# Layer 1's input projection by seven products of quarters in place of eight

## The chip, the cores and the metric

The kernel runs on one core of a Trainium2 chip. The metric is the device time of one execution in microseconds (us), the median of several runs; lower is better. A trace of one execution, taken by the profiler of the hardware, stands beside it.

## What is computed

Two layers of a diffusion trunk over L = 1024 tokens with D = 2048 channels, in float32. Layer 0 is an attention layer, layer 1 a pooling layer. Cut to what the change touches, layer 1 is:

```python
h = _rmsnorm(x, pre_g) * (1 + scale) + shift                 # (1024, 2048)
proj = h @ w_in                                              # w_in: (2048, 4096)
# four groups of 512 channels: centred means over 2, 4, 8, 16 tokens minus the token
pooled = multiscale(proj[..., :2048])
mixed = einsum('blgc,gcd->blgd', pooled, pool_w) * pool_scale  # pool_w: four of (512, 512)
y = mixed * silu(proj[..., 2048:])
x = x + gate * _rmsnorm(y @ w_out, post_g)
```

The first 2048 columns of `w_in` give the values, the last 2048 the gates.

## The kernel before, in words

Every float32 product is made of three TensorE passes over a high and a low part (`PASSES`): `split` casts a tile to the high part on ScalarE (L144) and subtracts it on VectorE for the low part (L147). Weights come by `w_tiles` as raw tiles `wr` of 512 KB (two buffers, SP's DMA queue), each split into two tiles `wh`, `wl` (four buffers of each); a matmul multiplies a 128x128 block of weights with 512 tokens and adds into one PSUM bank `g`. `load` is a DMA on SP's queue, `store` one on ScalarE's. GpSimd (POOL) issues no DMA and no DMA accumulates. A scheduler orders the instructions of each engine from the program's order and its own estimate of times; places named `pin` or `keep_in_program_order` are held.

Layer 0's attention runs in 32 units: 16 of dense attention, then 16 of windowed. Each unit loads `qt`, `zt` and, by way of DRAM (`lsd`), a broadcast of its row sums `rs`; GpSimd multiplies `zt` by `rs` (L857), VectorE multiplies the output by that (`y`, L863), and the result goes to DRAM (`yd`).

Layer 0's output projection (`out_proj`, L953) runs over two halves n of 512 tokens. After each half, its rows are normalised (`add_norm`), transposed (L1053), scaled (`nw`) and split into 16 operand tiles `hT[k][n]`. While the second half is normalised, TensorE works on `first_gates`: the gates of six blocks of 128 columns for the first half of the tokens (`BRIDGE`, 288 matmuls, L1034), with the transposes between them, and their SiLU goes to DRAM (`sd`).

Then, for each of four groups of 512 channels: `project1` makes the values of two blocks of 128 columns at a time, for both halves of the tokens (L184, names `g`), `pooled` makes the centred means of them (adds on VectorE and GpSimd in turn, L1097), `project1` makes the gates, the group's product with `pool_w` (`mx`, L184) is multiplied by the SiLU of the gates (L1128), and the result `yt` goes to DRAM. Layer 1's output projection follows (L953).

## Time and profile before

| | us |
|---|---|
| median of 3 runs | 3043.45 (3042.88 to 3043.84) |
| the profiled execution | 3042.5 |
| its span, first to last instruction | 3040.8 |
| TensorE busy | 2951.6 (97%), 14038 matmuls |
| VectorE busy | 1612.4 (53%) |
| ScalarE busy | 1067.0 (35%) |
| GpSimd busy | 169.3 (6%) |

The busy times are those of the span of the profiled execution; engines work side by side, so they don't add up to it. The DMA share is the mean busy share of the core's 16 DMA engines.

### The profile page before, as it was taken

To read this page: it belongs to the slowest core of one execution; us is meant where nothing else is said; L and a number is where in the kernel's file an instruction comes from. 1 tells how busy PE (TensorE), PEld (TensorE's weight loads), DVE (VectorE), ACT (ScalarE), POOL (GpSimd) and SP (SyncE) were. 2 spreads that over 40 slices of the span, in tenths; PEclk is the share of its full clock that TensorE was granted. 3 is DMA by queue.
4 is the path that set the end of the run, shared out by engine and by line. 5 is a ranking of instruction groups with operands and counts; after the bars stand their busy time and mean duration, and the time that the engine had idled before them with its cause. 6 is when DMAs were issued, how large, how long until landed. Compare 5 with 4: busy or idle time off the path is not lost.

```text
span 3040.8 us, 38187 instructions
## 1 busy us (share of the span) xinstructions
PE 2951.6 (97%) x14038; PEld 2456.4 (81%) x14038; DVE 1612.4 (53%) x2866; ACT 1067.0 (35%) x2060; POOL 169.3 (6%) x150
## 2 busy tenths in 40 slices
PE   5999999999999999999899999999999999999998
PEld 4788888778887878888778888888888888888887
DVE  7979875663347478888633543533333323233434
ACT  5553322211212267766632443522222212122322
POOL 0000000000000000002200210300000002000000
PEclk8999999999999999999999999999999999999999
DMA  8858878886668554446554635414122121454634
GB/s 314 291 179 258 257 238 260 280 291 218 210 220 298 178 151 142 115 150 167 143 188 157 237 97 170 150 49 143 45 95 76 63 90 49 151 191 146 252 109 163
DMA packets 373009, 530.32 MB, mean 174 GB/s; under 512 B 28644, under 2 KB 215894, under 8 KB 371670
## 3 DMA queue, kind: packets, MB, share of 16 engines
q1 hardware_dynamic: 287990, 445.81, 45.5%
q10 hardware_dynamic: 84832, 82.07, 7.9%
q8 instruction: 110, 1.80, 0.2%
q14 instruction: 77, 0.63, 0.1%
HBM read 428.88 MB, written 98.91 MB: 174 GB/s over the span
## 4 chain that ended last, share of the span: by engine, by line
PE 80%; DMA 11%; DVE 5%; issue 2%; ACT 1%; POOL 0%; SPq 0%; ACTq 0%; DVEq 0%; POOLq 0%
PE g L184 41%; PE g L953 21%; DMA mraw<-in_od_mod_w_dram 5%; PE o L895 4%; PE mx L184 3%; PE s L252 3%; PE t L841 3%; DVE mac L345 2%; PE g L1034 2%; DMA mraw<-in_ev_mod_w_dram 2%; DMA lsd<-ls 1%; DMA rs<-lsd 1%; DMA wr<-in_od_w_out_dram 1%; PE c L258 1%; DMA zt<-in_ctx_dram 1%
## 5 line engine op out<-in xcount | busy, mean ns | idle before, releaser
L147 DVE TENSOR_TENSOR wl<-wr,wh 128x512 fp32r<-128x512 f32 (+1 forms) x576 | 395.8, 692 | 843.2 <-ACT wh L144 831.1
L144 ACT CAST wh<-wr 128x512 fp32r<-128x512 f32 (+1 forms) x576 | 350.5, 616 | 1152.3 <-PE g L184 584.3
L184 PE MATMUL g<-h,wh 128*128 128x512 f32 x2368 | 743.0, 394 | 1.9 <-ACT h L144 1.8
L953 PE MATMUL g<-wh,a 128*128 128x512 f32 x1920 | 593.7, 390 | 0.4 <-ACT wh L144 0.4
L184 PE MATMUL g<-a,wh 128*128 128x512 f32 x1856 | 571.2, 389 | 0.0
L184 PEld LDWEIGHTS g<-h,wh 128*128 128x128 f32 x2368 | 445.3, 190 | 93.6 <-ACT h L144 2.5
L184 PE MATMUL g<-h,wl 128*128 128x512 f32 x1184 | 465.0, 393 | 5.0 <-DVE wl L147 5.0
L953 PEld LDWEIGHTS g<-wh,a 128*128 128x128 f32 x1920 | 360.2, 188 | 75.1 <-ACT wh L144 0.8
L345 DVE SCALAR_TENSOR_TENSOR mac<-mraw,csil,mac 128x512 f32<-128x512 f32 x480 | 357.1, 748 | 112.6 <-DMA mraw<-in_od_mod_w_dram 61.1
L184 PEld LDWEIGHTS g<-a,wh 128*128 128x128 f32 x1856 | 348.4, 188 | 72.3
L953 PE MATMUL g<-wl,a 128*128 128x512 f32 x960 | 373.7, 389 | 0.0
L184 PE MATMUL g<-a,wl 128*128 128x512 f32 x928 | 360.7, 389 | 0.0
L184 PEld LDWEIGHTS g<-h,wl 128*128 128x128 f32 x1184 | 224.4, 190 | 53.0 <-DVE wl L147 6.5
L953 PEld LDWEIGHTS g<-wl,a 128*128 128x128 f32 x960 | 180.2, 188 | 37.5
L184 PEld LDWEIGHTS g<-a,wl 128*128 128x128 f32 x928 | 174.2, 188 | 36.3
L147 DVE TENSOR_TENSOR tl<-t,th 128x512 fp32r<-128x512 f32 x236 | 160.0, 685 | 39.2 <-ACT th L144 37.8
L144 ACT CAST th<-t 128x512 fp32r<-128x512 f32 x236 | 135.9, 585 | 111.3 <-PE t L841 110.3
L895 PE MATMUL o<-th,vt 128*128 128x512 f32 x472 | 156.2, 412 | 2.5 <-ACT th L144 2.5
L841 PE MATMUL t<-ident,p 128*128 128x128 f32 x944 | 138.9, 276 | 10.2 <-DVE tl L147 9.8
L841 PEld LDWEIGHTS t<-ident,p 128*128 128x128 f32 x944 | 114.4, 141 | 38.1 <-DVE tl L147 15.6
L857 POOL TENSOR_TENSOR zt<-zt,rs 128x512 f32<-128x512 f32 x32 | 49.6, 1552 | 1426.0 <-DMA zt<-zd 1075.5
L252 PE MATMUL s<-kt,qt 128*128 128x512 f32 x384 | 103.4, 404 | 0.0
(216 smaller groups left out, 3002.6 us busy)
## 6 DMA issues: line engine op xcount, KB each, us to landing
mraw<-in_ev_mod_w_dram SPq DMA_DIRECT2D x192, 256.0 KB, 4.2
mraw<-in_od_mod_w_dram SPq DMA_DIRECT2D x192, 256.0 KB, 4.2
wr<-in_od_w_in_dram SPq DMA_DIRECT2D x76, 512.0 KB, 3.7
wr<-in_ev_w_in_dram SPq DMA_DIRECT2D x68, 512.0 KB, 4.7
mraw<-in_ev_mod_w_dram SPq DMA_DIRECT2D x64, 512.0 KB, 4.7
wr<-in_ev_w_out_dram SPq DMA_DIRECT2D x64, 512.0 KB, 3.7
wr<-in_od_w_out_dram SPq DMA_DIRECT2D x64, 512.0 KB, 5.2
qd<-hl ACTq DMA_DIRECT2D x64, 256.0 KB, 3.9
```

What stands on the lines that cost most here:

```text
L144: nc.scalar.copy(dst_h, src)
L147: (lo or nc.vector).tensor_tensor(dst_l, src, f32(dst_h), op=ALU.subtract)
L184: pin(nc.tensor.matmul(o, lhsT=w[a][:, kk, m * P : (m + 1) * P], rhs=rhs(n, k, b), start=(k == 0 and i == 0), stop=(k == kc - 1 and i == 2),))
L252: pin(nc.tensor.matmul(s[:, sl], lhsT=qt[:, h, a], rhs=kt[:, b, sl], start=i == 0, stop=i == 2))
L258: pinned(nc.tensor.matmul(cs[:, hh], lhsT=qt[:, h + hh, a], rhs=kt[:, b, L:], start=i == 0, stop=i == 2))
L345: nc.vector.scalar_tensor_tensor(a, w, c, a, op0=ALU.mult, op1=ALU.add)
L841: pin(nc.tensor.transpose(t[:, h * P : (h + 1) * P], ps[h][:, i * P : (i + 1) * P], ident))
L857: GATE.tensor_tensor(zt, zt, rs.rearrange("p q h -> p h q"), op=ALU.mult)
L895: pin(nc.tensor.matmul(outs[u], lhsT=vt[:, a, kb], rhs=b, start=(i == 0 and jj == 0), stop=(last and jj == 2)))
L953: nc.tensor.matmul(o, lhsT=y[k][:, a, t * P : (t + 1) * P], rhs=wt[b][:, k - k0, :], start=(k == 0 and i == 0), stop=(k == KC - 1 and i == 2),
L1034: mm = nc.tensor.matmul(o, lhsT=w[a][:, k - k0, m * P : (m + 1) * P], rhs=hT[k][0][:, b], start=(k == 0 and i == 0), stop=(k == KC - 1 and ...
```

## The change

One level of a seven-product scheme (Strassen's, with Winograd's sums) replaces the eight products of layer 1's input projection. The tokens' channels are cut into X11, X12 (first 512 tokens; channels 0 to 1023 and 1024 to 2047) and X21, X22 (last 512 tokens), the weights into W11, W12, W21, W22 (channels by values or gates). `quarter(a, b, q, c)` is 512 KB of W: four 128-row blocks of half q of row quarter a, 256 columns of block c of column quarter b. Each product is 1024 channels x 2048 columns x 512 tokens.

- `early_sums`, in the attention units: for the first four of eight column blocks c and both q, sums of quarters of W11, W12 and W22 are made by DMA (load one quarter, then `accum_op=add` DMAs on GpSimd's queue) and stored to DRAM as `td` (three quarters) and `te` (two quarters),; every sign of the scheme is in the sums of tokens.
- `first_products` takes the place of `first_gates`: X11 W11 goes into PSUM, is copied out (`p1d`), and X12 W21 goes on top of it; the result `ud` is the values of the first 512 tokens. Two quarters of weights (24 matmuls) stand between two transposes. Four VectorE subtractions per channel block make the operand tiles of the later products; three of the five are spilled to DRAM (`opd`).
- `second`, a stage with its own pool and a ring of six raw tiles: product 3 with W12+W11+W22 (`td`), minus `p1d`, is stored as `u2d`; product 4 with W22+W12 (`te`) goes on top in PSUM, minus `p1d`, is stored as `u3d`. For c from 4 on the sums are made here.
- The third stage reloads three sets of eight operand tiles (`reloaded`), and makes for each group the values of the last 512 tokens (X22 with `td`+W21), the gates of the last and, on top in PSUM, those of the first 512 tokens. The product with `pool_w` of a group runs after the values of the next group, for each half of the tokens apart, so `pool_w` is loaded twice. All pooling adds are VectorE's.
- Layer 0's first half of the output projection casts its operand tiles on ScalarE, no longer on GpSimd, and stores them to DRAM as `xd` too.

```diff
+OG = 16
+EARLY = 4
+BETWEEN = 2
+PL = 3
+RING = 6
...
+    w_in1 = ins["od_w_in"][0]
+    def quarter(a, b, q, c):
+        r = (8 * a + 4 * q) * P
+        return w_in1[r : r + 4 * P, b * D + c * 256 : b * D + (c + 1) * 256].rearrange("(k p) m -> p k m", p=P)
...
+        early = []
+        def early_sums(u):
+            c, q, step = u // 8, u // 4 % 2, u % 4
+            if c >= EARLY:
+                return
+            dma = nc.gpsimd.dma_start
+            if step == 0:
+                early[:] = [ap.tile([P, 4, 256], F32, tag=tag, name=tag, bufs=1) for tag in ("qa", "qb")]
+                for r, b in zip(early, (0, 1)):
+                    load(r, quarter(b, 1, q, c))
+            elif step == 1:
+                for r, b in zip(early, (0, 1)):
+                    dma(out=r, in_=quarter(0, b, q, c), accum_op=ALU.add)
+            elif step == 2:
+                load(te[q][c], early[1])
+                dma(out=early[0], in_=quarter(1, 1, q, c), accum_op=ALU.add)
+            else:
+                load(td[q][c], early[0])
...
+            early_sums(u)
...
+    raw_tiles = [lambda: wp.tile([P, 1024], F32, tag="wr", name="wr", bufs=2)]
+    raws_made, ring = [0], [2]
+    def quarter_tiles(src):
+        for q in range(2):
+            i = raws_made[0] % ring[0]
+            raws_made[0] += 1
+            raw = raw_tiles[i > 1]()
+            r = raw.rearrange("p (k m) -> p k m", k=4)
+            first, *others = src(q)
+            load(r, first)
+            for o in others:
+                if o[0] == "store":
+                    store(o[1], r)
+                else:
+                    nc.gpsimd.dma_start(out=r, in_=o[1], accum_op=ALU.add)
+            for i in range(2):
+                h = wp.tile([P, WT], F32R, tag="wh", name="wh", bufs=WB)
+                l = wp.tile([P, WT], F32R, tag="wl", name="wl", bufs=WB)
+                split(h, l, raw[:, i * WT : (i + 1) * WT])
+                yield 4 * q + 2 * i, 2, [t.rearrange("p (k m) -> p k m", k=2) for t in (h, l)]
+    def sum_of(c, *quarters, kept=None, more=None):
+        def at(q):
+            r = [quarter(a, b, q, c) for a, b in quarters]
+            if more:
+                r.insert(0, more[q][c])
+            return [r[0], *(("add", o) for o in r[1:]), *([("store", kept[q][c])] if kept else [])]
+        return at
+    def products(outs, group, op, first, pin=lambda i: i):
+        for m, o in enumerate(outs):
+            for k0, nk, w in group:
+                for k in range(k0, k0 + nk):
+                    for i, (a, b) in enumerate(PASSES):
+                        pin(nc.tensor.matmul(
+                            o, lhsT=w[a][:, k - k0, m * P : (m + 1) * P], rhs=op(k)[:, b],
+                            start=(first and k == 0 and i == 0), stop=(k == 7 and i == 2), skip_group_check=not first,
+                        ))
...
+        def first_products():
+            def part(c, outs, i):
+                for k0, nk, w in quarter_tiles(sum_of(c, (i, 0))):
+                    products(outs, [(k0, nk, w)], lambda k: hT[8 * i + k][0], i == 0, tc.keep_in_program_order)
+                    yield
+            def evicted(c, outs, d):
+                for m, o in enumerate(outs):
+                    t = ev.tile([P, HL], F32, tag="pe", name="pe", bufs=2)
+                    nc.scalar.copy(t, o)
+                    store(d[2 * c + m], t)
+            held = {}
+            for c in range(9):
+                if c < 8:
+                    held[c] = [psg.tile([P, HL], F32, tag="g", name="g") for _ in range(2)]
+                    yield from part(c, held[c], 0)
+                    evicted(c, held[c], p1d)
+                if c:
+                    outs = held.pop(c - 1)
+                    yield from part(c - 1, outs, 1)
+                    evicted(c - 1, outs, ud)
...
+        early = first_products()
+        list(islice(early, LEAD))
+        ops = [[None] * 8 for _ in range(2)]
+        for k in range(8):
+            x11 = ev.tile([P, HL], F32, tag="x11", name="x11", bufs=2)
+            x12 = ev.tile([P, HL], F32, tag="gp", name="x12", bufs=1)
+            load(x11, xd[k])
+            load(x12, xd[k + 8])
+            ws = []
+            for kk in (k, k + 8):
+                list(islice(early, BETWEEN))
+                ws.append(columns_of(1, kk, og))
+            x21, x22 = ws
+            s3 = ev.tile([P, HL], F32, tag="s3", name="s3", bufs=1)
+            nc.vector.tensor_tensor(s3, x21, x11, op=ALU.subtract)
+            nc.vector.tensor_tensor(x21, x21, x22, op=ALU.subtract)
+            nc.vector.tensor_tensor(x11, x11, x21, op=ALU.subtract)
+            nc.vector.tensor_tensor(x12, x12, x11, op=ALU.subtract)
+            for i, a in enumerate((x11, s3)):
+                ops[i][k] = acts[1, i].tile([P, 2, HL], F32R, tag="a", name="a")
+                operand(ops[i][k], a)
+            for i, a in enumerate((x22, x21, x12)):
+                store(opd[i][k], a)
+        list(early)
...
+        ready = [fetched(p1d[m]) for m in range(2)]
+        def second(c, outs, accumulate):
+            if c < EARLY:
+                src = sum_of(c, more=(td, te)[accumulate])
+            else:
+                src = sum_of(c, (1, 1), (0, 1)) if accumulate else sum_of(c, (0, 1), (0, 0), (1, 1), kept=td)
+            product(outs, src, ops[accumulate], not accumulate)
+            for m, o in enumerate(outs, 2 * c):
+                p = ready.pop(0) if ready else fetched(p1d[m])
+                nc.vector.tensor_tensor(p, o, p, op=ALU.subtract)
+                store((u2d, u3d)[accumulate][m], p)
+        held = {}
+        for c in range(9):
+            if c < 8:
+                held[c] = pair()
+                second(c, held[c], 0)
+            if c:
+                second(c - 1, held.pop(c - 1), 1)
...
+        def reloaded(i, n, half):
+            r = []
+            for k in range(8):
+                t = acts[n, half].tile([P, 2, HL], F32R, tag="a", name="a")
+                w = fetched(opd[i][k])
+                split(t[:, 0], t[:, 1], w)
+                r.append(t)
+            return r
+        x22, s1t, s4t = reloaded(0, 1, 0), reloaded(1, 0, 0), reloaded(2, 0, 1)
...
+        def values(g, c2):
+            c, outs = 2 * g + c2, pair()
+            product(outs, sum_of(c, (1, 0), more=td), x22)
+            r = []
+            for m, o in enumerate(outs, 2 * c):
+                u = us[m % 2]
+                load(u[:, PAD : PAD + HL], ud[m])
+                nc.vector.tensor_tensor(u[:, PAD + HL : PAD + L], o, fetched(u3d[m]), op=ALU.subtract)
+                r.append(pooled(g, m, u))
+            return r
+        def gates(g, c2, outs, n):
+            c = 2 * g + c2
+            if n:
+                product(outs, sum_of(c, (0, 1), (0, 0)), s1t)
+            else:
+                product(outs, sum_of(c, (1, 1)), s4t, False)
+            for m, o in enumerate(outs, 2 * c):
+                p = fetched((u2d, u3d)[n][m])
+                nc.vector.tensor_tensor(p, o, p, op=ALU.add)
+                nc.scalar.activation(p, p, AF.Silu)
+                store(sd[m][n], p)
...
+        mixes = []
         for g in range(4):
+            po = values(g, 0) + values(g, 1)
+            for f in mixes:
+                f()
+            held = [pair(), pair()]
+            for n in (1, 0):
+                for c2 in range(2):
+                    gates(g, c2, held[c2], n)
+            mixes = [lambda g=g, cc=cc, n=n, po=po: mixed(g, cc, n, po) for n in range(NH) for cc in (0, 2)]
+        for f in mixes:
+            f()
```

GpSimd's queue at the start of the dense attention units, before (only the products of `zt` and `rs`):

```order
L857 TENSOR_TENSOR zt_9186<-zt_9186,rs_8993 128x512 [waits DMAHW0_49,DMAHW7_49,DVE_49,PE_49]
L857 TENSOR_TENSOR zt_9400<-zt_9400,rs_9219 128x512 [waits DMAHW6_49]
L857 TENSOR_TENSOR zt_9615<-zt_9615,rs_9434 128x512 [waits DMAHW4_49,DMAHW3_49,DVE_49]
```

Each row is one unit's product. With the change, in the same place (the DMA rows accumulate into `qa` and `qb`):

```order
L896 TENSOR_TENSOR zt_9340<-zt_9340,rs_9147 128x512 [waits DMAHW1_49,DMAHW2_49,DVE_49,PE_49]
L864 DMA qa_9368<-in_od_w_in_dram 128x4x256 [waits DMAHW3_49,DVE_49]
L864 DMA qb_9369<-in_od_w_in_dram 128x4x256 [waits DMAHW4_49,DVE_49,PE_49]
L867 DMA qa_9368<-in_od_w_in_dram 128x4x256 [waits DMASW0_49]
L864 DMA qb_10237<-in_od_w_in_dram 128x4x256 [waits DMAHW5_49,DMAHW3_49,DMASW1_49]
L896 TENSOR_TENSOR zt_9558<-zt_9558,rs_9377 128x512 [waits DMAHW4_49,DMAHW1_49]
L864 DMA qa_10236<-in_od_w_in_dram 128x4x256 [waits DMAHW5_49,DMAHW1_49,DMASW2_49]
L867 DMA qa_10236<-in_od_w_in_dram 128x4x256 [waits DMASW4_49]
L864 DMA qb_11112<-in_od_w_in_dram 128x4x256 [waits DMAHW6_49,DMAHW0_49,DMASW3_49]
L896 TENSOR_TENSOR zt_9775<-zt_9775,rs_9594 128x512 [waits DMAHW1_49,DVE_49]
```

Three accumulating DMAs and one product of a unit now alternate in one queue, and the second DMA into the same buffer waits for the first.

SP's queue in the second dense unit and after it, before (issued loads and stores of the attention):

```order
L240 DMA qt_9621<-qd0_1_109 128x1024 [waits DMAHW0_49,PE_49]
L856 DMA zt_9830<-zd0_0_116 128x512 [waits DMAHW1_49,DVE_49]
L287 DMA lsd2_126<-ls_9194 128x4 [waits DMAHW2_49,DVE_49,Activation_49]
L867 DMA yd0_0_156<-yo_9423 512x1x128 [waits DMAHW3_49,Activation_49]
L909 DMA rs_9434<-lsd2_126 128x512 [waits DMAHW2_49]
L867 DMA yd0_0_156<-yo_9423 512x1x128 [waits DMAHW5_49,DVE_49]
```

The unit's own transfers follow one another. With the change, the same place reads:

```order
L259 DMA qt_9564<-qd0_0_108 128x1024 [waits DMAHW4_49,PE_49]
L866 DMA te0_0_196<-qb_9369 128x1024 [waits DMAHW5_49,DMASW1_49]
L895 DMA zt_9775<-zd0_0_116 128x512 [waits DMAHW6_49,DVE_49]
L306 DMA lsd1_125<-ls_9169 128x4 [waits DMAHW7_49,DVE_49,Activation_49]
L906 DMA yd0_0_156<-yo_9363 512x1x128 [waits DMAHW0_49,Activation_49]
L869 DMA td0_0_180<-qa_9368 128x1024 [waits DMAHW1_49,DMASW2_49]
L906 DMA yd0_0_156<-yo_9363 512x1x128 [waits DMAHW2_49,DVE_49]
L861 DMA qb_10237<-in_od_w_in_dram 128x4x256 [waits DMAHW5_49,DMAHW3_49]
L948 DMA rs_9377<-lsd1_125 128x512 [waits DMAHW7_49,DMAHW4_49]
L861 DMA qa_10236<-in_od_w_in_dram 128x4x256 [waits DMAHW1_49]
L866 DMA te1_0_200<-qb_10237 128x1024 [waits DMAHW6_49,DMASW3_49]
```

The stores of `te` and `td` and the loads of the next quarters now stand between `zt`, `lsd`, `yd` and `rs`, and each waits for a DMA of GpSimd's queue (DMASW) or for a buffer.

SP's queue around the load of `edge`, where layer 1's groups begin, before:

```order
L160 DMA wr_18148<-in_od_w_in_dram 128x4x256 [waits DMAHW1_49,DVE_49]
L160 DMA wr_18206<-in_od_w_in_dram 128x4x256 [waits DMAHW6_49,DMAHW2_49,DVE_49]
L1067 DMA edge_18023<-in_edge_dram 128x64 [waits DMAHW7_49]
L1127 DMA zt_18760<-sd0_180 128x512 [waits Pool_49]
L160 DMA wr_18298<-in_od_w_in_dram 128x4x256 [waits DMAHW3_49,DVE_49]
L160 DMA wr_18356<-in_od_w_in_dram 128x4x256 [waits DMAHW6_49,DVE_49]
```

The weight loads of the first group run on through it. With the change, at the start of the third stage (`pl` from `opd` are the reloads of X22's operand tiles, from `p1d` those of the second stage):

```order
L1062 DMA wr_20527<-td0_0_180 128x1024 [waits DMASW6_49,DVE_49]
L1195 DMA pl_20389<-p1d15_259 128x512 [waits DMAHW6_49,DMAHW5_49,DVE_49]
L1062 DMA wr_20562<-td1_0_188 128x1024 [waits DMASW7_49,DVE_49]
L1062 DMA wr_20745<-in_od_w_in_dram 128x4x256 [waits DMAHW1_49,DMASW0_49,DVE_49]
L1062 DMA wr_20780<-in_od_w_in_dram 128x4x256 [waits DMAHW4_49,DMASW1_49,DVE_49]
L1232 DMA edge_20397<-in_edge_dram 128x64 [waits DMAHW2_49]
L1195 DMA pl_20406<-opd0_0_220 128x512 [waits DMAHW6_49,DMASW5_49,DMASW2_49]
L1195 DMA pl_20411<-opd0_1_221 128x512 [waits DMAHW7_49,DMASW3_49]
L1195 DMA pl_20416<-opd0_2_222 128x512 [waits DMAHW0_49]
L1286 DMA u0_20399<-ud0_292 128x512 [waits DMAHW3_49,DMAHW1_49]
```

The reloads of X22 now stand behind four loads of weight tiles into two `wr` buffers.

## Rows read from the trace of the kernel before

**Rows 1.** The page: the span, TensorE's busy time, the 40 slices of clock and DMA.
```profile
span 3040.8 us, 38187 instructions
PE 2951.6 (97%) x14038; PEld 2456.4 (81%) x14038; DVE 1612.4 (53%) x2866; ACT 1067.0 (35%) x2060; POOL 169.3 (6%) x150
...
PEclk8999999999999999999999999999999999999999
DMA  8858878886668554446554635414122121454634
```

**Rows 2.** The chain that ended last, from 1888 us: start us, us, what.
```profile
1888.50 39.44 PE g L1034 x174
1928.38 1.38 PE g L1034 x6
...
1962.72 107.21 PE g L184 x473
2069.94 11.19 PE mx L184 x48
2081.13 21.77 PE g L184 x96
...
2681.81 85.03 PE g L953 x375
```

**Rows 3.** Windows: stretch, its us, busy us (instructions) by engine, clock, DMA share, GB/s.
```profile
1093.00:1260.00 167.00, 166.36 (x950) 137.63 (x949) 139.54 (x241) 118.25 (x242) 13.99 (x9) 1.00 0.44 127
1888.50:2069.90 181.40, 181.40 (x833) 150.38 (x833) 83.37 (x170) 72.40 (x137) 28.41 (x34) 1.00 0.32 104
1888.50:2681.80 793.30, 793.30 (x3521) 655.01 (x3521) 274.23 (x463) 207.18 (x360) 66.58 (x66) 1.00 0.29 95
2300.00:2320.00 20.00, 20.00 (x90) 16.56 (x89) 2.07 (x3) 1.47 (x4) 0.00 (x0) 1.00 0.18 53
```

**Rows 4.** The page: SP's DMA queue: packets, MB, share of 16 engines' span.
```profile
q1 hardware_dynamic: 287990, 445.81, 45.5%
```

**Rows 5.** DMA issues: out<-in, queue, number, KB each, median us to landing.
```profile
wr<-in_od_w_in_dram SPq DMA_DIRECT2D x76, 512.0 KB, 3.7
qt<-qd SPq DMA_DIRECT2D x32, 512.0 KB, 8.5
...
y1d<-yt ACTq DMA_DIRECT2D x32, 512.0 KB, 2.6
...
rs<-lsd SPq DMA_DIRECT2D x32, 256.0 KB, 3.7
zt<-zd SPq DMA_DIRECT2D x32, 256.0 KB, 3.0
...
zt<-sd SPq DMA_DIRECT2D x6, 256.0 KB, 4.6
```

**Rows 6.** Timeline of SP, one issue in an attention unit: start us, us, what.
```profile
1096.77 0.32 SPq L909 DMA_DIRECT2D rs<-lsd  x1
```

**Rows 7.** Timeline of VectorE, the gated outputs of two attention units.
```profile
1111.42 0.68 DVE L863 TENSOR_TENSOR y<-o,zt 128x512 f32<-128x512 f32 x1
...
1129.93 0.68 DVE L863 TENSOR_TENSOR y<-o,zt 128x512 f32<-128x512 f32 x1
```

**Rows 8.** Timeline of GpSimd (POOL) in the same units.
```profile
1100.24 1.56 POOL L857 TENSOR_TENSOR zt<-zt,rs 128x512 f32<-128x512 f32 x1 [22.70 <-DMA rs<-lsd]
1120.35 1.55 POOL L857 TENSOR_TENSOR zt<-zt,rs 128x512 f32<-128x512 f32 x1 [18.55 <-DMA rs<-lsd]
```

**Rows 9.** Groups by line and shape: shapes, count, busy us, mean ns, idle before.
```profile
L147 DVE TENSOR_TENSOR wl<-wr,wh 128x512 fp32r<-128x512 f32 x544 | 378.1, 700 | 835.8 <-ACT wh L144 823.8 <-DMA a<-y1d 8.8 <-DMA hc<-hcd 0.9
L144 ACT CAST wh<-wr 128x512 fp32r<-128x512 f32 x544 | 334.3, 622 | 1101.0 <-PE g L184 553.1 <-PE g L953 305.3 <-DMA wr<-in_ev_w_out_dram 49.3
...
L1128 DVE SCALAR_TENSOR_TENSOR zt<-mx,v,zt 128x512 f32<-128x512 f32 x32 | 24.0, 751 | 39.9 <-PE mx L184 31.6 <-DMA zt<-sd 7.4 <-ACT zt L1080 0.9
L1097 DVE TENSOR_TENSOR s<-u 128x543 f32<-128x543 f32 x32 | 23.1, 721 | 40.1 <-ACT u L1087 39.4
```

More of the change, by code (lines that the diff above doesn't have):

```diff
@@ L45 @@
 LAST = "TTPATTAPTPPTTPATPTPTPPNP"
-BRIDGE = 6
 PINS = (0,)
@@ new lines, in operand @@
+        def operand(o, w):
+            split(o[:, 0], o[:, 1], w)
+        og = out_proj(ev, ins["ev_w_out"][0], ys[0], gpd[0], 0, lambda t: x[t * P : (t + 1) * P, :], add_norm, other_half(yd))
+        for k in range(KC):
+            w = columns_of(0, k, og)
+            store(xd[k], w)
+            hT[k][0] = act_tile(k, 0)
+            operand(hT[k][0], w)
+        og = out_proj(ev, ins["ev_w_out"][0], ys[1], gpd[0], 1, lambda t: x[t * P : (t + 1) * P, :], add_norm)
+        early = first_products()
@@ new lines, in tile_backbone, with etile, fetched, pair @@
+        list(early)
+    with ExitStack() as st:
+        s_two = st.enter_context(ExitStack())
+        ev = pool(s_two, "ev2a")
+        raw_tiles.append(lambda: ev.tile([P, 1024], F32, tag="wr2", name="wr2", bufs=RING - 2))
+        raws_made[0], ring[0] = 0, RING
+        def etile(tag, bufs):
+            return ev.tile([P, HL], F32, tag=tag, name=tag, bufs=bufs)
+        def fetched(d, tag="pl", bufs=PL):
+            t = etile(tag, bufs)
+            load(t, d)
+            return t
+        def pair():
+            return [psg.tile([P, HL], F32, tag="g", name="g") for _ in range(2)]
+        def product(outs, src, op, first=True):
+            for group in twos(quarter_tiles(src)):
+                products(outs, group, lambda k: op[k], first)
+        ready = [fetched(p1d[m]) for m in range(2)]
[16 more added lines that the diff above has]
+                second(c - 1, held.pop(c - 1), 1)
+        s_two.close()
@@ L1065, in tile_backbone @@
         ev = pool(st, "ev2")
+        raw_tiles[1] = lambda: ev.tile([P, 1024], F32, tag="wr2", name="wr2", bufs=2)
+        raws_made[0], ring[0] = 0, 4
         edge = ev.tile([P, 64], F32, name="edge")
```

127 lines of the change are left out of this document (49 added, 78 removed).

## The prediction

> **What bounds the kernel now.** The page comes first: TensorE is busy for 97% of the span, the granted clock stands at 9 or more of 10 in every slice but the first, and the DMA line sits at 1 to 5 tenths where layer 1 runs [rows 1]. The reader should see that nothing but matmul time counts there. The chain that ended last says the same piece by piece: from 1888.50 to 2681.81 us it is TensorE without a break, first the bridge of gates (L1034) with the transposes (L1053) between, then the projections (L184) and the group products (mx, L184), and at 2681.81 the output projection [rows 2]. The windows confirm it: in these 793.3 us TensorE is busy for all 793.30, VectorE for 274, ScalarE for 207, GpSimd for 67, the DMA engines for 0.29 [rows 3]. So a matmul taken out here is worth its full time, as long as what is put in fits beside. The stage is rich in everything but TensorE, and the change spends just that.
>
> **What it removes.** One product of 512 tokens, 1024 channels and 2048 columns is 16 column blocks x 8 channel blocks x 3 passes = 384 matmuls; eight of them are 3072, which is the bridge's 288 and the 2784 left to L184, and seven are 2688. A projection matmul takes 21.77 / 96 = 0.2268 us (107.21 / 473 = 0.2267) [rows 2]. 384 x 0.2267 = 87.05 us go. The mx matmuls (384, at 11.19 / 48 = 0.233) and the 64 transposes stay. The four products that go on top of others in PSUM add no instruction of their own to TensorE. The profiled execution took 3042.5 us (span 3040.8 and 1.7 around it), the median of the runs is 0.95 above it. With nothing late the median would be 3043.45 - 87.05 = 2956.4.
>
> **The price of an accumulating DMA.** No row of before shows one. Below it is the plain load of the same quarter, 3.7 us from issue to landing for 512 KB [rows 5]. It must also read what it adds to, so above I take a load and a store of that size, 3.7 + 2.6 = 6.3 us [rows 5], and twice the engine time. In engine time SP's queue moved 445.81 MB at 45.5% of 3040.8 us, so 322 GB/s if all 16 engines were busy [rows 4]; a stretch with weight loads alone gives 53 / 0.18 = 294 [rows 3]. 0.524 MB then cost 1.6 us of all engines once, 3.3 twice. I take a third of the way (4.6 us, and 1.33 times a load), since the row that it is nearest to is the load: same source, same tile, and no byte more from DRAM. The Trainium skill, "DMA: Bandwidth & Descriptors", section "Anatomy of one DMA — SWDGE (gpsimd) path", gives 2.0 us and bytes over 436 GB/s for a transfer issued by GpSimd, 3.2 us here as an estimate; it does not say whether adding costs more, and no run here shows it yet. By it the attention term below would be near nothing.
>
> **Attention: eight cycles of quarter sums.** Each of eight (c, q) takes two loads, three accumulating DMAs and two stores, seven transfers of 512 KB; the order packs them into some nine units, where POOL had only its zt, and SP's qt, zt, lsd, rs and yd. All is in order on two queues, and the buffers qa and qb are single, so a cycle is a chain: load 3.7, add, add, store 2.6, and some 0.35 us each to issue, from SP's 0.32 [rows 6]. At 4.6 us an add that is 16.9 us, at 6.3 it is 20.3, and a unit lasts 18.5 (y at 1111.42 and 1129.93) [rows 7]. POOL's zt ends at 1101.80 and 1121.90 and is wanted at the next y [rows 7, 8], so 8 to 9.6 us can be lost once. In latency it fits at my price; at 6.3 it loses 8 x 1.8 - 8 = 6 us. Volume is tighter: 56 x 0.524 = 29.4 MB are 91 us of all engines, and these nine units (1093 to 1260, 167 us) already use 0.44, 74 us [rows 3]: 165 of 167. At 1.33 the 24 adds cost 13 us more, 178, so 11 over, of which the free half of the units on either side and the 8 us of slack take back a part. I book **6 us** (0 to 35). The Trainium skill says in the same page, section "Issuing engines are not separate DMA queues", that transfers from any engine run on the same 16 engines and interleave, so POOL's queue brings no bandwidth. That speaks against the change here and in the two stages below; the rows here don't test it, since no stretch of them is full.
>
> **First products** (P1 and then P2 on top, 768 matmuls, 174 us). Quarters come as plain loads, 32 in 174 us, one per 5.44 us at 3.7 of landing; the spills (x11, x12 loads, three stores per k, p1d and ud) fit. Four VectorE differences at 0.7 and two splits per k, where two splits were, lie in a window of 181 us with 83 of VectorE [rows 3]. 24 matmuls stand between two transposes, against 6 before [rows 2]. ScalarE gets 32 evictions, a cast's 0.62 each [rows 9], and loses the 32 of u: with 72 of 181 us busy [rows 3] it hides them. In the first half of layer 0's output projection it takes 16 casts over from POOL, and the stores of xd; if nothing hid these it would be 16 x 0.62 = 10 us, but these tiles are wanted only when the second half's output projection is through, so I count nothing. **2 us** (0 to 8).
>
> **Second stage** (products 3 and 4, 768 matmuls). For c below 4 the sums are ready: four loads, four p1d loads, four stores per c, 4.2 MB, 13 of 21.77 us of TensorE. From c = 4 on it is 4 loads, 6 adds, 2 td stores, 4 p1d loads and 4 stores, 8.4 MB, 26 us at plain price, 29 at 1.33, 36 at 2, beside 21.77: over by 4, 7.5 or 14 us per c, four times 17, 30 or 56. Six raw buffers let the loads run ahead by about four quarters of 5.44 us, 22 us. Left over: 0, **8**, 34 us.
>
> **Start of the third stage.** SP has two weight loads (wr) in front of the reloads of x22. The second wr waits for a split that needs a weight tile which TensorE gives back with its last product. Then: split 1.3 us (0.62 + 0.70 [rows 9]), two issues, the reload of 256 KB (4.6 as zt from sd [rows 5]), a cast and a subtract, 8 us in all before the first matmul; the other seven come through three buffers, three per 6.2 us, and k = 6 is 5 us late again. **12 us** (5 to 18).
>
> **Third stage**, per group 288 + 96 matmuls, 87.7 us. Transfers: 12 quarter loads, 8 adds, 4 pool_w loads, 32 of 256 KB and 8 stores of yt: 25.2 MB, 78 us at plain price, 82.5 at 1.33, 91 at 2. VectorE, group 3: 32 weight tiles at 0.70 (22), 12 sums (8), 32 adds at 0.72 (23; half of them were POOL's), 32 more of pooling and y at 0.70 to 0.75 (23), edges (3): some 79 us of 87.7 [rows 9]. Both are close, both have cover from one group to the next. The mixed products of the group before run behind the values, so pooling has a stage to hide in. **5 us** in all (0 to 20).
>
> **Sum**: 2956.4 + 6 + 2 + 8 + 12 + 5 = 2989.4; I say **2990**, -53.
>
> **The rivals.** (a) All transfers are hidden, and only the head of the third stage stays: 2956 + 5 to 9, 2961 to 2965, gain 79 to 82. For it: shares of 0.29 before; against: three places that are computed at 0.9 of the engines or more. Chance 0.17. (b) Mine, between 2966 and 3020: 0.48. (c) Part of the way, 3020 to 3037, with an adding DMA near 1.7: 0.09. (d) No change, within 0.2% (6 us, about what a measurement of this kernel can tell from none): the stalls eat the 87 just so, 0.05. (e) **Slower**: the single pair qa, qb. The cycle holds POOL's zt and SP's lsd and rs in order behind it, so every us over 18.5 + slack is TensorE's wait. Losses elsewhere are 27, so it takes 60 in attention: 8 x (T - 18.5) - 8 = 60 gives a cycle T of 27, or 6.4 us as the mean of its four transfers. qt from qd, 512 KB too, took 8.5 in this very stretch [rows 5]; at 8.5 T is 35.4, the loss 127, the time 2956 + 27 + 127 = 3110. Against it: rs and zt, in the same units, land in 3.7 and 3.0 for 256 KB [rows 5]. With an engine time of twice for each add, the second stage (34) and the third (13) push the same way. 3050 to 3110, chance 0.21. That the change does less than it says is no rival: the order shows 384 matmuls fewer.
>
> **The numbers.** Faster by over 0.2% are (a), (b) and (c), 0.74; same 0.05; slower 0.21. Eight in ten: from 2958, below (a)'s time with a margin for a head that is hidden too, to 3055, the low edge of (e). For (b) alone it would be 2968 to 3018.
>
> **What would show it.** TensorE's matmul count down by 384 at 0.2267 us each; in the attention units, zt on POOL later than 10 us after the y before it, or not; the landing of the adding DMAs at 4.6 us, or at 3.7 or above 6.4; TensorE idle for about 12 us on an operand tile at the head of the third stage; gaps on wh or wl in the second stage only from c = 4 on. The prediction is wrong if the adding DMAs take 6.4 us or more (then slower), if they cost no more than a load (then (a)), or if the idle time stands at a place that I priced at 2 to 5 us: the first products or the groups.

## The result, and the profile after

The changed kernel is slower: 3113.41 us in the median (3110.53 to 3116.63) against 3043.16 of before, a ratio of 1.0231 (95% interval 1.0213 to 1.0249). The likeliest forecast was 2990, the range 2958 to 3055. The product went as planned (384 matmuls fewer), and some 160 us of waiting and slower matmuls came with it.

The page after, with the rows that answer to [rows 1] and [rows 4] (q0 is GpSimd's queue, the accumulating DMAs; packets, MB, share of 16 engines' span):

```profile
span 3113.6 us, 38864 instructions
PE 2900.6 (93%) x13654; PEld 2406.0 (77%) x13654; DVE 1762.1 (57%) x3126; ACT 1141.2 (37%) x2202; POOL 209.5 (7%) x164
...
PEclk8999999999999998899999999999898999999999
DMA  8857877885678599645554654677998998974634
...
q1 hardware_dynamic: 333014, 528.14, 52.0%
...
q0 software_dynamic: 42240, 41.95, 8.7%
```

TensorE has 384 matmuls fewer but only 51 us less of busy time, at 93% of a longer span, and behind the first slice its granted clock leaves 9 tenths at two places: 1168 to 1323 us (attention) and in two slices between 2180 and 2413 (the second stage and the head of the third). The DMA row is at 6 to 9 in these slices, where it stood at 1 to 4 before. And q0 is dear: 41.95 MB in 8.7% of 3113.6 us are 155 GB/s, where q1's 528.14 MB in 52.0% are 326.

The windows of after, as in [rows 3] (attention's first nine units; then first products, second stage, head of the third stage, its rest, the four of them together; then the output projection):

```profile
1093.00:1260.00 167.00, 132.78 (x705) 109.92 (x704) 104.88 (x177) 88.14 (x181) 33.57 (x25) 0.91 0.97 244
...
1941.20:2122.40 181.20, 181.20 (x833) 150.12 (x832) 98.07 (x186) 90.12 (x173) 18.15 (x16) 1.00 0.66 215
2122.40:2330.50 208.10, 183.34 (x770) 148.48 (x768) 59.80 (x92) 37.66 (x64) 33.28 (x26) 0.94 0.93 243
2330.50:2400.00 69.50, 39.01 (x148) 30.63 (x149) 29.09 (x49) 22.40 (x39) 7.79 (x7) 0.83 0.91 239
2400.00:2748.50 348.50, 328.62 (x1390) 267.11 (x1390) 233.46 (x391) 121.09 (x207) 30.66 (x24) 0.97 0.92 270
1941.20:2748.50 807.30, 732.17 (x3138) 596.34 (x3137) 420.42 (x716) 271.26 (x482) 89.89 (x72) 0.96 0.86 248
2748.50:3113.60 365.10, 351.98 (x1536) 289.62 (x1535) 138.18 (x256) 102.84 (x204) 0.00 (x0) 0.98 0.53 178
```

Attention is measured by POOL's first and last zt, before and then after:

```profile
1075.99 1.55 POOL L857 TENSOR_TENSOR zt<-zt,rs 128x512 f32<-128x512 f32 x1 [1075.55 <-DMA zt<-zd]
1529.28 1.56 POOL L857 TENSOR_TENSOR zt<-zt,rs 128x512 f32<-128x512 f32 x1 [0.69 <-DMA rs<-lsd]
```

```profile
1075.82 1.56 POOL L896 TENSOR_TENSOR zt<-zt,rs 128x512 f32<-128x512 f32 x1 [1075.37 <-DMA zt<-zd]
1583.99 1.56 POOL L896 TENSOR_TENSOR zt<-zt,rs 128x512 f32<-128x512 f32 x1 [0.89 <-DMA rs<-lsd]
```

Stage by stage, in us; a stage of layer 1 ends with its own last matmul:

| | before | after | matmuls alone | lost |
|---|---|---|---|---|
| attention, first zt to last zt | 453.3 | 508.2 | | 54.9 |
| first products and transposes | | 181.2 | 181.1 | 0 |
| second stage | | 208.1 | 174.1 | 34.0 |
| third stage | | 418.0 | 350.7 | 67.3 |
| all of layer 1's projection | 793.3 | 807.3 | 706.3 | 101.0 |
| layer 1's output projection to the end | 359.0 | 365.1 | | 6.1 |

"Matmuls alone" is the stage's matmuls and transposes at the times of before; 706.3 is 793.3 less the 87.05 taken out; 359.0 is from 2681.8 [rows 2] to the end of the span. With 2 us gained between attention and layer 1, 54.9 + 14.0 + 6.1 - 2.2 are the 72.8 by which the span grew (3040.8 to 3113.6). Of the 101.0 us, 75.1 are idle time of TensorE (732.17 of 807.3 busy) and 25.9 are matmuls that took longer than 0.2267: in the head the granted clock was 0.83, a mix of both levels (1.2 and 2.4 GHz), behind waits of up to 14.6 us. Some expectations below count 116 us here and 25 in the second stage: their projection ends at 2763 us, behind 53 matmuls (12.0 us) of the output projection, and at 2320 the second stage had 43 of its 768 matmuls still to come.

The adding DMAs themselves, from the issues (queue, number, KB, median us to landing):

```profile
wr<-in_od_w_in_dram POOLq DMA_DIRECT2D x56, 512.0 KB, 9.8
...
qa<-in_od_w_in_dram POOLq DMA_DIRECT2D x16, 512.0 KB, 7.7
...
qa<-in_od_w_in_dram SPq DMA_DIRECT2D x8, 512.0 KB, 4.9
...
te<-qb SPq DMA_DIRECT2D x8, 512.0 KB, 5.9
```

An add lands in 7.7 us in attention and 9.8 in layer 1, not 4.6. What that does in attention stands in SP's timeline of one unit (start us, us, what):

```profile
1139.36 0.38 SPq L895 DMA_DIRECT2D zt<-zd  x1
1153.44 0.32 SPq L869 DMA_DIRECT2D td<-qa  x1
1153.87 0.45 SPq L306 DMA_DIRECT2D lsd<-ls  x1
...
1159.50 0.54 SPq L948 DMA_DIRECT2D rs<-lsd  x1
```

and GpSimd's and VectorE's, where that unit's product and output follow (`ls` on VectorE is what lsd is made from):

```profile
1147.59 1.28 POOL L867 DMA_DIRECT2D qa<-in_od_w_in_dram  x1 [8.67 <-DMA qa<-in_od_w_in_dram]
...
1163.68 1.51 POOL L896 TENSOR_TENSOR zt<-zt,rs 128x512 f32<-128x512 f32 x1 [13.51 <-DMA rs<-lsd]
```

```profile
1138.48 0.17 DVE L305 RECIPROCAL ls<-ls 128x4 f32<-128x4 f32 x1
...
1165.23 0.69 DVE L902 TENSOR_TENSOR y<-o,zt 128x512 f32<-128x512 f32 x1 [8.32 <-POOL zt L896]
```

The second add into qa is issued at 1147.59 and lands 5.8 us later; only then does SP get to store td, and the row sums (lsd) of the unit stand right behind that store, although they had been ready since 1138.65. SP issued nothing between 1139.7 and 1153.44. Then lsd, rs, zt and y follow in line: y comes at 1165.23, 28.0 us after the one before it, where [rows 7] had 18.5.

### The profile page after: what moved, and what is told of

The parts are those of the page before. It is cut to its first block, busy times and chain, and to the rows that moved or that the text cites. A ratio compares the mean times of both kernels' runs of the same rounds, so it can differ in the third digit from the quotient of the medians.

```text
span 3113.6 us, 38864 instructions
## 1 busy us (share of the span) xinstructions
PE 2900.6 (93%) x13654; PEld 2406.0 (77%) x13654; DVE 1762.1 (57%) x3126; ACT 1141.2 (37%) x2202; POOL 209.5 (7%) x164
## 3 DMA queue, kind: packets, MB, share of 16 engines
q1 hardware_dynamic: 333014, 528.14, 52.0%
q0 software_dynamic: 42240, 41.95, 8.7%
## 4 chain that ended last, share of the span: by engine, by line
PE 38%; DMA 13%; DVE 3%; issue 2%; ACT 1%; POOL 1%; SPq 0%; ACTq 0%; DVEq 0%; POOLq 0%
PE g L993 21%; PE g L1089 10%; DMA wr<-in_od_w_in_dram 5%; PE o L934 2%; PE t L880 1%; DMA lsd<-ls 1%; DMA wr<-td 1%; PE s L271 1%; DMA rs<-lsd 1%; DMA pl<-opd 1%; DMA sd<-pl 1%; DMA pl<-u2d 1%; DVE wl L166 1%; DMA y1d<-yt 1%; PE g L1311 0%
## 5 line engine op out<-in xcount | busy, mean ns | idle before, releaser
L166 DVE TENSOR_TENSOR wl<-wr,wh 128x512 fp32r<-128x512 f32 (+1 forms) x664 | 448.5, 683 | 757.3 <-ACT wh L163 710.1
L163 ACT CAST wh<-wr 128x512 fp32r<-128x512 f32 (+1 forms) x664 | 399.6, 615 | 1133.0 <-PE g L993 284.4
L993 PEld LDWEIGHTS g<-wl,a 128*128 128x128 f32 x960 | 181.1, 189 | 40.9 <-DVE wl L166 3.2
L934 PEld LDWEIGHTS o<-th,vt 128*128 128x128 f32 x472 | 79.9, 195 | 63.9 <-issue 50.9
```

The source lines that it names most:

```text
L163: nc.scalar.copy(dst_h, src)
L166: (lo or nc.vector).tensor_tensor(dst_l, src, f32(dst_h), op=ALU.subtract)
L934: pin(nc.tensor.matmul(outs[u], lhsT=vt[:, a, kb], rhs=b, start=(i == 0 and jj == 0), stop=(last and jj == 2)))
L993: nc.tensor.matmul(o, lhsT=y[k][:, a, t * P : (t + 1) * P], rhs=wt[b][:, k - k0, :], start=(k == 0 and i == 0), stop=(k == KC - 1 and i == 2),
```

## The experiments

Times of before differ from chip to chip (3037 to 3046 us), so each run is read beside the run of before on its own chip. Runs 1 to 9 are single executions, and seven executions of before on one chip lay between 3033.27 and 3044.88: a difference of some 12 us or less between two single times shows nothing by itself, and the stages in the traces are the better evidence.

**1. The adds as plain transfers.**

```diff
-                    dma(out=r, in_=quarter(0, b, q, c), accum_op=ALU.add)
+                    dma(out=r, in_=quarter(0, b, q, c))
...
-                    nc.gpsimd.dma_start(out=r, in_=o[1], accum_op=ALU.add)
+                    nc.gpsimd.dma_start(out=r, in_=o[1])
```

> The 80 accumulating DMAs become plain ones on the same queue, from the same places into the same tiles (so the sums of weights are not formed). Theory 1, the price of adding: in the changed kernel GpSimd's queue moved 41.95 MB in 8.7% of 16 engines' span, 155 GB/s, where SP's moved 528.14 MB in 52.0%, 326 GB/s. Plain, the queue should go at about 300 GB/s and give back some 140 us of engine time; the 53 us lost in attention should fall below 15, the 116 us that layer 1's projection stage stands over its matmuls' 706 should fall by half, and the time to 3000 to 3020. Theory 2, order and volume: the extra transfers stand in order before zt, lsd and rs whatever they do, so the attention keeps 40 us or more of its loss and the time stays above 3080.

3032.22 beside 3037.01. The queue after, and the windows of the nine units and of layer 1's projection:

```profile
q0 software_dynamic: 11520, 41.95, 4.2%
```

```profile
1093.00:1260.00 167.00, 151.58 (x828) 125.36 (x827) 122.02 (x210) 103.18 (x211) 26.61 (x28) 0.94 0.87 281
1918.80:2668.00 749.20, 718.34 (x3138) 586.84 (x3137) 420.79 (x715) 272.69 (x481) 60.16 (x72) 0.98 0.79 267
```

The same bytes on the same queue took 4.2%, 330 GB/s: GpSimd's queue is no slower than SP's, it is the adding that takes the engines 2.1 times as long (144 us of all 16 engines over the run). The projection's loss fell from 101.0 to 42.9 us, by over half, as theory 1 had it. The attention (1084.2 to 1560.9) still lost 23.5, and the time too lies between what the two theories gave: order and volume hold a part of it.

**2. No adds at all.**

```diff
-                for r, b in zip(early, (0, 1)):
-                    dma(out=r, in_=quarter(0, b, q, c), accum_op=ALU.add)
+                pass
...
-                dma(out=early[0], in_=quarter(1, 1, q, c), accum_op=ALU.add)
...
-                else:
-                    nc.gpsimd.dma_start(out=r, in_=o[1], accum_op=ALU.add)
```

> The 80 accumulating DMAs are left out (the sums of weights are not formed), all else stays. Theory 1: 271 us of engine time go, the attention loses under 5 us, and what is left over 2956 is the head of the third stage and the spills: 2975 to 3000. Theory 2 gives the same for the attention, but then the step from plain transfers to none is the large one, 60 us or more; by theory 1 it is 10 to 25.

2989.56 beside 3037.01. The same two windows, and between them the head of the third stage, up to its 176th matmul:

```profile
1093.00:1260.00 167.00, 158.59 (x886) 130.58 (x885) 131.71 (x228) 110.47 (x226) 12.32 (x8) 0.98 0.72 223
2252.90:2312.00 59.10, 44.41 (x175) 35.99 (x176) 31.13 (x53) 24.00 (x41) 0.00 (x0) 0.86 0.69 227
1897.20:2628.60 731.40, 712.01 (x3138) 586.88 (x3137) 423.99 (x718) 274.66 (x483) 18.17 (x16) 0.99 0.70 234
```

The attention loses 5.4 us, the projection 25.1. From plain transfers to none it was 43 us, again between the two theories' 10 to 25 and 60. So of the projection's 101.0 us some 58 are the price of adding, 18 are 56 further transfers of any kind, and 25 were there without a single add: none of them in the second stage (174.5 us for 174.1), 19 in the head of the third, which lasts 59.1 us for the 39.9 of its matmuls, and some 5 in the groups behind it.

**3. No sums in attention.**

```diff
-EARLY = 4
+EARLY = 0
```

> No sums in attention (EARLY = 0); the second stage makes them for all eight column blocks. Theory 1: the 53 us of the attention come back, and the second stage has for each of eight blocks 5.2 MB at 326 and 3.1 MB at 155 GB/s, 36 us of engines for 21.8 us of matmuls, so it loses 8 x 14.6 less a lead of 22, 95 us, where it now loses 25: about 3130. Theory 2: the attention is freed and the second stage, where no zt waits, takes the plain price, 26 us a block, 10 us lost: about 3050.

3108.23 beside 3037.01. The attention came back whole (450.6 us from first to last zt), and the projection took 865.4 us, 58.1 more than with early sums; theory 1 had said 70. In the second stage the engines are full (by its packets' times, 1.07 of 16 engines):

```profile
2061.00:2335.00 274.00, 196.08 (x772) 154.44 (x770) 65.63 (x104) 41.04 (x70) 64.47 (x50) 0.86 1.07 253
```

Where the sums are made moves the loss, 55 us there or 58 here, and does not end it.

**4. Adds beside an idle DMA.** The kernel before, with this at the head of each of layer 1's groups:

```diff
+            qs = ev.tile([P, 4, 256], F32, tag="qs", name="qs", bufs=1)
+            load(qs, w_in1[0 : 4 * P, 0:256].rearrange("(k p) m -> p k m", p=P))
+            for i in range(1, 7):
+                nc.gpsimd.dma_start(out=qs, in_=w_in1[0 : 4 * P, i * 256 : (i + 1) * 256].rearrange("(k p) m -> p k m", p=P), accum_op=ALU.add)
```

> The kernel before, with one load and a chain of six accumulating DMAs of 512 KB into a tile of its own at the head of each of layer 1's four groups, where the DMA engines are 0.2 to 0.3 busy; nothing reads the tile. Theory 1: an adding DMA lands in 5 to 7 us even alone, and the queue shows about 155 GB/s. Theory 2: it lands in about 4, near a load's 3.7, at some 300 GB/s, and the 7.7 to 9.8 of the changed kernel are queueing. Time within 2 us of before by both.

The median landing is 5.9 us, and the queue:

```profile
q0 software_dynamic: 12672, 12.58, 2.7%
```

That is 152 GB/s with room around it, so the price in engine time is the operation's and not the crowd's; the landings of 7.7 to 9.8 us in the changed kernel have the crowd in them too. But the time was 3076.63 beside 3037.01, which neither theory had said. The chain shows it:

```profile
1971.11 5.91 DMA qs<-in_od_w_in_dram
1977.31 5.74 DMA qs<-in_od_w_in_dram
...
2091.21 4.86 DMA wr<-in_od_w_in_dram
2096.84 7.68 PE g L184 x24
```

The second group's load of qs waited in SP's queue until the first group's six adds were through, and the weight loads stood behind it: 30 us of idle TensorE from 24 transfers that nobody read. It is the unit of attention above in a second place.

**5. What an add is dear by.** The kernel before, with one chain that nothing waits for, four of each kind:

```diff
+            for r in (1, 2, 4, 1):
+                t = spare if r == 4 else spare.rearrange("p (k m) -> p k m", k=4 // r)
+                for i in range(4):
+                    nc.gpsimd.dma_start(out=t, in_=rows[r], accum_op=ALU.add)
+            for i in range(4):
+                nc.gpsimd.dma_start(out=spare.rearrange("p (k m) -> p k m", k=4), in_=rows[1])
```

> The kernel before with one chain of 20 DMAs of 512 KB on GpSimd's queue in layer 1's projections, none beside another and none that another engine waits for: four accumulating with source rows of 1 KB, four with 2 KB, four with 4 KB, four with 1 KB again, then four plain ones of 1 KB rows. Theory 1a, adding costs by bytes (each byte of the destination is read too): the 16 adding ones take the same 5.8 us each whatever the rows, the plain ones 4 or less. Theory 1b, adding costs by packet: an accumulating DMA of 1 KB rows went in 528 packets and a plain one in 144; with rows of 4 KB the adding one should come near the plain one, 4 to 4.5 us. Time of the kernel within 5 us of before by both.

3042.64 beside 3038.19. GpSimd's timeline (in brackets the idle time before, which is the wait for the DMA before it): adds with 2 KB rows, with 4 KB rows, with 1 KB rows, then plain ones:

```profile
2000.34 1.20 POOL L1119 DMA_DIRECT2D spare<-in_od_w_in_dram  x1 [5.73 <-DMA spare<-in_od_w_in_dram]
...
2031.18 0.86 POOL L1119 DMA_DIRECT2D spare<-in_od_w_in_dram  x1 [4.81 <-DMA spare<-in_od_w_in_dram]
...
2062.50 1.28 POOL L1119 DMA_DIRECT2D spare<-in_od_w_in_dram  x1 [4.89 <-DMA spare<-in_od_w_in_dram]
...
2072.95 0.76 POOL L1121 DMA_DIRECT2D spare<-in_od_w_in_dram  x1 [3.51 <-DMA spare<-in_od_w_in_dram]
```

The wait behind an add is 4.7 to 6.1 us with 2 KB rows, 4.7 to 5.0 with 4 KB and 4.8 to 6.5 with 1 KB, behind a plain DMA 3.5 to 4.6; rows of 4 KB save 0.4 us of issue. Theory 1b fails: with rows of 4 KB an add still takes 5.6 to 5.9 us from one issue to the next, not 4 to 4.5. What is left is theory 1a; that the price grows with the bytes is not shown, since all 20 moved 512 KB.

**6. Sums in SBUF by GpSimd.** No DMA accumulates, none is made in attention; the second stage makes W12+W22 once for both products.

```diff
+                nc.gpsimd.tensor_tensor(ra, ra, rt, op=ALU.add)
+                nc.gpsimd.tensor_tensor(rb, rb, ra, op=ALU.add)
...
-                    nc.gpsimd.dma_start(out=r, in_=o[1], accum_op=ALU.add)
+                    w = raw_tiles[-1]()
+                    load(w.rearrange("p (k m) -> p k m", k=4), o[1])
+                    nc.gpsimd.tensor_tensor(raw, raw, w, op=ALU.add)
```

> No DMA accumulates and no sums are made in attention: the second quarter is loaded plain and GpSimd adds it in SBUF (128x1024, about 3.1 us by twice the 1.55 of zt). The second stage shares the sum W12+W22 between its two products and so needs three loads and two adds per quarter where it had five transfers, 6.3 MB a block, 20 us of engines beside 21.8 of matmuls, and takes product 4 right after product 3 of the same block; the third stage has the plain volume, 78 us of 87.7 a group, and two raw tiles fewer in flight by one. Theory 1: attention back to before, second stage hidden, 15 to 45 us left over in the third stage: 2970 to 3000 against 3043 of before. Theory 2: in-order queues with few buffers lose as much with any engine that adds, or GpSimd's and VectorE's adds slow each other: 3030 or more.

3029.67 beside 3038.19, at most a small gain where 40 to 70 was hoped for, and by its time at theory 2's bound. An add took GpSimd 2.4 to 2.5 us. The chain at the head of its third stage:

```profile
2272.88 5.39 DMA pl<-opd
...
2279.67 4.69 DMA pl<-opd
...
2287.56 4.71 DMA pl<-opd
```

All 24 reloaded operand tiles go through three buffers in turn, 6 to 9 us a link, from 2273 to 2322 us, with the u3d loads behind them that free PSUM.

**7 and 8. The reload straight into its tile**, on the changed kernel and on the version of run 6:

```diff
-                w = fetched(opd[i][k])
+                w = f32(t)[:, 1]
+                load(w, opd[i][k])
                 split(t[:, 0], t[:, 1], w)
```

> The changed kernel, with one thing else: the 24 operand tiles of the third stage are loaded straight into the low half of their tiles and split in place there, not by way of three pl buffers. If the head of the third stage was the 24 reloads in line (three buffers, some 6.5 us a round, with the u3d loads behind them), 20 to 30 us come back there and the time falls to 3080 to 3095 beside 3113. If it was the weight loads in front of them in SP's queue, or the DMA engines full of adds, it stays within 8 us of 3113.

> GpSimd's sums in SBUF as in the run before (3029.7 beside 3038.2), with the direct reload too. By theory 1 the rest of its loss is at the head of the third stage (some 50 us from the last product of the second stage, 20 of them idle, and a lowered clock behind): 3000 to 3015. By theory 2 the reloads only move to where other transfers stand: above 3022.

3096.79 and 3028.01, beside 3046.01: a ratio of 1.0167 where the changed kernel has 1.0231, and 0.9941 where run 6 had 0.9972. The changed kernel's projection went from 807.3 to 791.0 us, a little under the 20 to 30 expected. The second run missed its 3000 to 3015 and came out as theory 2 had it: the loads of the second and third operand set now crowd the start of the second stage, which lost 17 us of 50.

**9. The same adds, spread.** On the changed kernel, the 24 adds and the products of zt held in the program's order on GpSimd:

```diff
-                    dma(out=r, in_=quarter(0, b, q, c), accum_op=ALU.add)
+                    pin(dma(out=r, in_=quarter(0, b, q, c), accum_op=ALU.add))
...
-                dma(out=early[0], in_=quarter(1, 1, q, c), accum_op=ALU.add)
+                pin(dma(out=early[0], in_=quarter(1, 1, q, c), accum_op=ALU.add))
...
-            GATE.tensor_tensor(zt, zt, rs.rearrange("p q h -> p h q"), op=ALU.mult)
+            pin(GATE.tensor_tensor(zt, zt, rs.rearrange("p q h -> p h q"), op=ALU.mult))
```

> The changed kernel, with the 24 accumulating DMAs of the attention held in the program's place on GpSimd's queue: one step of a quarter's cycle a unit, over all 32 units, where the order had packed them into the first nine dense ones. Same transfers, same prices. In the nine units the DMA engines stood at 0.97 busy. If it was a full set of engines there (132 us of transfers for 93 us of room), spreading them gives back 40 us or more of the 53 and the time is 3060 to 3075 beside 3113. If it was the order of the queues (zt behind an add that waits for a landing of 7.7 us), each unit still has such an add and 25 us or more stay lost: 3085 or above.

3101.39 beside 3037.46. The attention took 491.9 us, so 16 of its 54.9 came back and 38.7 stayed lost, as the second theory had it. The two halves of attention tell why (dense units, then windowed ones):

```profile
1085.00:1389.00 304.00, 294.01 (x1672) 244.15 (x1671) 246.41 (x435) 205.26 (x425) 40.05 (x28) 0.98 0.67 183
1389.00:1577.00 188.00, 147.99 (x869) 127.46 (x867) 114.42 (x296) 107.18 (x264) 57.69 (x42) 0.90 0.76 192
```

The dense half took 304 us from zt to zt with four cycles in it, 296.6 before: 1.9 us a cycle, where the packed order paid 55 / 8 = 6.9. There the crowding was the larger part; whether by the full set of engines or by three adds in one unit's queue, this run does not tell. The windowed half took 188 us instead of 157, with the other four cycles in it: its units are chains of lsd, rs, zt and yd already, and what stands beside them shows.

**10 and 11. The first block early, loads pinned; two staging tiles.** Of the lines shown, the first is against the changed kernel and the others are against run 8; run 11 has two `ws` tiles in place of one besides.

```diff
+                pin(dma(out=early[0], in_=quarter(1, 1, q, c), accum_op=ALU.add))
...
-                load(r.rearrange("p (k m) -> p k m", k=4), v)
+                tc.keep_in_program_order(load(r.rearrange("p (k m) -> p k m", k=4), v))
...
-                load(w, opd[i][k])
+                tc.keep_in_program_order(load(w, opd[i][k]))
```

> GpSimd's sums in SBUF and the direct reload, as in the run that took 3028.0 beside 3046.0, with two things else: the first column block's sums are made in attention (two cycles of DMAs, spread), so that the second stage can start on ready sums, and the reloads of the second and third operand sets are held behind the sums of blocks 2 and 4. The start of the second stage lost 17 us of 50 there (DMA 0.97). If that comes back: 2.0 to 3.0% under before in neither case more than the matmuls' 87 us, so a ratio of 0.985 to 0.990. If the loss moves to the next block, 0.993 to 0.996.

> The same with two staging tiles for the third stage's sums in place of one, and one less of zt and pl for it. In the run at 3028.0 the chain at the head of the third stage was load, add, load, add (3.6 and 2.4 us each), some 10 us of idle TensorE. If one staging tile was the limit, 5 to 10 us under the run beside it; if GpSimd or VectorE is, or pl is short now, no better, within 3 us or slower.

1.0086 (1.0062 to 1.0109) and 1.0136 (1.0114 to 1.0158): both missed, some 1% slower than before. SP's timeline of run 10:

```profile
2111.67 6.04 SPq L1214 DMA_DIRECT2D wr<-in_od_w_in_dram  x6
2117.81 22.62 SPq L1196 DMA_DIRECT2D pl<-p1d  x4
2140.48 3.94 SPq L1235 DMA_DIRECT2D a<-opd  x8
2144.51 6.99 SPq L1214 DMA_DIRECT2D wr<-in_od_w_in_dram  x6
```

With the raw loads pinned, four p1d loads stand as a block between two blocks' weights and wait, up to 16.3 us at once, for pl tiles that the stores of u2d give back; SP issues no weights from 2117.7 to 2144.5. Run 11 shares the pins; why it is slower still stays open.

**12 and 13. Without the pins, timed.**

> The version with GpSimd's sums in SBUF and the direct reload again, timed. One look gave a ratio of 0.9941. If that was no chance: 0.992 to 0.997, faster than before and 2.5 to 3% faster than the changed kernel. If it was the chip's scatter, the interval holds 1.

> The same with the first block's sums made by two spread cycles of DMAs in attention, and without pins on layer 1's loads. If the pins lost the time in e10 (p1d loads in front of raw loads in SP's queue), this one gets back part of the 17 us at the start of the second stage: 5 to 15 us under e12. If the early block loses it (td and te through two wr buffers, then a late second block), it is 10 us or more over e12.

Run 12, which is the kernel of run 8, has a ratio of 0.9964 (0.9950 to 0.9978), run 13, with the first block's sums made by two spread cycles in attention, 0.9946 (0.9931 to 0.9962), a median of 3028.06 beside 3042.33. That is faster than both kernels, than the one before by 14 us or half a per cent, and than the changed one by some 85 us. Run 13 is run 10 without the pins on layer 1's loads, so these pins had lost the time, and not the early block. Whether the early block gains anything is not shown: the intervals of 12 and 13 overlap, the 4 us between their medians are short of the 5 to 15 expected, and run 13 also has two sets of reloads earlier in the program. The projection of run 13:

```profile
1893.60:2665.90 772.30, 725.10 (x3138) 586.23 (x3137) 477.12 (x716) 269.07 (x482) 167.68 (x76) 0.98 0.77 255
```

It is still 66 us over its matmuls' 706.3, with the DMA engines at 0.77.

## Why the prediction was wrong, step by step

- **What bounds the kernel, what is removed**: right. TensorE lost 384 matmuls, and where it was fed they took 0.2267 us (the first products: 181.2 us for 181.1).
- **The price of an accumulating DMA: the step that failed first.** I took 4.6 us and 1.33 loads of engine time, "since the row that it is nearest to is the load". It is 5.9 us with room around it (run 4) and 2.1 loads of engine time, the latter just over my upper bound, and 7.7 to 9.8 us where it ran. That is over the 6.4 us which I had named as a sign of being wrong. The Trainium skill ("DMA: Bandwidth & Descriptors", "Anatomy of one DMA — SWDGE (gpsimd) path") gives 3.2 us, as an estimate from its fit, for a transfer on that queue. It holds for neither kind here: in run 5 the next issue came 5.6 to 7.7 us after that of an add, and 4.3 to 5.3 after that of a plain transfer.
- **Attention, 6 us booked (0 to 35), 55 measured: the largest miss.** The chain of rival (e) was the right one, and its own formula gives the size: load 4.9, two adds of 7.7, a store of td not listed with a landing (te's took 5.9), 1.4 of issue are 27.6; 8 x (27.6 - 18.5) - 8 = 65. Runs 1 and 2 divide it: 5 us for loads and stores, 18 for 24 more transfers, 31 for adding. The rival's total, 3110, was met by chance: it had 127 us in attention and 27 elsewhere, and it was 55 and some 105.
- **Issuing engines share the DMA engines** (the Trainium skill, same page, "Issuing engines are not separate DMA queues"): the trace agrees. Nine units stood at 0.97 and the second stage at 0.93, 1.07 in run 3, and SP's own loads of w_in landed in 6.0 us in the median of after, 3.7 before [rows 5].
- **First products, 2 booked**: 0. **Second stage, 8 booked (0 to 34)**: 34.0, the bound of two loads an add. The adding is the cause: the stage took 208.1 us here, 180.2 with plain transfers (run 1) and 174.5 with none (run 2).
- **Head of the third stage, 12 booked (5 to 18)**: 69.5 us with 148 matmuls, 36 lost. The mechanism that I named (weight loads in front in SP's queue) is there, and the first wait, 14.6 us for an operand tile, is the one that I priced at 12. But I priced the three buffers for the eight tiles of X22 alone, and 24 go through them with the u3d loads behind: two more waits for operand tiles took 5.8 us, and one for u, which needs u3d, 9.9. The chain of after has its links below; run 7 took 16 us of the projection back by the reload alone.
- **Rest of the third stage, 5 booked (0 to 20)**: 348.5 us in place of 317, 31 lost. At the true price its 88 us of matmuls a group stand beside 91 us of transfers, and I let two resources at 0.9 and over hide in each other. A stage at 0.92 of the DMA engines in the mean, with three pl tiles, four raw ones and landings of 4 to 14 us, had no slack to hide in; without adds (run 2) the groups behind the head lost some 5.
- **The clock was in no term.** 26 of the projection's 101 us are slower matmuls behind waits. Nor was the output projection in one, which lost 6 more.

So all terms but the first products came in at their upper bounds or over them. The price of adding is the larger part (58 of the projection's 101 us and 31 of the attention's 55), but not the whole: without a single add the head still lost 19 us, where I had booked 12.

The chain of after at the head of the third stage (start us, us, what):

```profile
2366.79 4.86 DMA pl<-opd
2373.04 5.08 DMA pl<-opd
2379.52 6.47 DMA pl<-opd
```

What stays open: how much of the attention's loss is full engines and how much is the order of GpSimd's queue, and whether the price of an add grows with its bytes.

## What to carry to other kernels

Where the matmul engine is fed without a break, price added transfers by the engine time of the stage in which they stand, and do not let a stage near 0.9 hide anything: here all stages at 0.9 or over lost time, and run 2's projection, at 0.70 in the mean, still lost 25 us. An operation that the trace does not show is priced at the worse bound, above all if it carries the change; one chain of it in the old kernel (run 5) gives its price. And a queue that issues in order passes on every wait: one store that waited for an add held up the row sums of attention, loads that waited for a free tile held up the weights.

## What the runs showed of the hardware

- An accumulating DMA from DRAM into SBUF, 512 KB, took 2.1 times the engine time of a plain one (155 and 152 GB/s against 330 on the same queue) and landed in 5.9 us in the median with room around it (run 4); source rows of 1, 2 or 4 KB made no difference of note, and a plain one on that queue takes the engines no longer than one of SP's (330 and 326 GB/s).
- GpSimd added 128x1024 float32 in SBUF in 2.4 to 2.5 us, less than the 3.1 that twice its product zt would give; VectorE's 632 subtractions of wl took 735 ns in the mean of run 6 and 690 in the changed kernel; that GpSimd's adds are the cause is not shown.
- In the head of the third stage, where TensorE was busy for 39.0 of 69.5 us and waited for up to 14.6 at once, the granted clock was 0.83; slower matmuls are a quarter of the projection's loss.
